# Gates of all rows at the end of the sample's attention, and the sample's recurrence products batch by batch

## The chip, the cores and the metric

The kernel runs on one core of a Trainium2 chip. What counts is the time of one execution on the device, in microseconds (us). The kernel before took 2453.69 us (median of 3 runs, 2449.02 to 2461.51).

The engines are named as the profile names them: PE (TensorE, matrix products; PEld its weight loads), DVE (VectorE), ACT (ScalarE), POOL (GpSimd) and SP (SyncE, which only starts DMA transfers here). Each works through its own queue in order and waits on semaphores for the others.

## What is computed

The reference is one inference step of a decoder layer for 256 prompt tokens and for a sample of 8 sequences with 4 new tokens each (288 rows in all, `NT`; 256 of them `NPR`). Cut to what matters here:

```python
# x @ w_in, split: RWKV-7 heads (16 x 64) | sparse attention heads (16 x 64, 4 KV heads)
g = jax.nn.sigmoid(gl) @ p['rwkv_g2']                    # gate, 160 -> 1024 columns
def step(S, inp):                                        # recurrence over tokens, S is 64 x 64 per head
    r_t, d_t, k_t, v_t, kk_t, a_t = inp
    sk = jnp.einsum('bhvk,bhk->bhv', S, kk_t)
    S = (S * d_t[:, :, None, :] - sk[..., None] * (kk_t * a_t)[:, :, None, :]
         + v_t[..., None] * k_t[:, :, None, :])
    return S, jnp.einsum('bhvk,bhk->bhv', S, r_t)
# y: group norm of the recurrence's rows, times g;  attention: compressed, selected and window branches
# x1 = LN1(ALPHA * x + concat(y, attention) @ w_out)
# PEER: q = x1 @ peer_wq, scores against two sets of 128 keys, the 16 best of the sums per head,
# out = sum over 8 heads x 16 experts of softmax * gelu(x1 . peer_u[e]) * peer_v[e];  LN2
```

## The kernel before

The code issues work in program order, and a scheduler with a cost model lays it out on the five queues. The function `weave` takes several generators, each with a number of units, and steps them in turn so that they advance in proportion; each generator says with `yield` where a unit ends. So the order around the change comes from the units given to `weave`, from buffer counts of the pools (a tile waits until the last reader of its buffer is done) and from `tc.issue_after(x)`, which ties instructions behind an instruction x in the schedule.

The stages, with the times that they have in the profile of before:

- **W3** (from about 575 to 758): `weave` of `late` (the sample's attention over its paged cache, 98 units: `sample_late`, in it 20 steps that load K and V into a ring of NCX = 10 buffers `co`, score, turn and apply them) with `sample_states` and `sample_steps` (54 units) and `outcomes`. `sample_states` loads the recurrent states of 8 sequences in two groups of four (16 DMAs each, L1240) and turns them (L1244) into `S0T`. `sample_steps` begins with the products of all states with the 4 tokens' rows, 128 small matmuls at L1259 (the profile records 256), copies them out in 16 pieces as `Ua` and `Ya`, solves the four steps, forms the new states (L1324 to L1327), turns them back (L1332) and writes them (L1337). The window's keys and values are loaded at L899.
- **W4** (to about 976): `weave` of the first units of `sample_chain`, of `prompt_attention` and of `out_first`. `sample_chain` multiplies the sample's gates (L1503, L1504), then its output product, its LN1, its wq and its scores with weights through a ring of NCW = 5 buffers `cw` (loads L1525, products L1527), and chooses its experts (L1362 to L1447). `prompt_attention` scores compressed blocks with small matmuls (L648) and then runs over blocks (scores L686, transposes L705, values L712, sums L717 and L721). `out_first` multiplies the prompt's gates (L1718 to L1720) and runs `out_part(0, BV)`, the half of the out product that takes the recurrence. The products of `out_part` are split into high and low parts: `YH`, `YL` (L1674, L1675) for the rows, `wh`, `wl` (L1684, L1685) for the weights, three matmuls each (L1690).
- **out** (to about 1059): the last units of `sample_chain` are `sample_dots`, NSD = 14 steps of two dots each: a gather of 128 half rows of an expert table (512 KB, POOL's queue, L453) into the ring `cw` and one DVE instruction (L1586). They are woven with `out_part(8, YN)`, the half that takes the attention.
- **ln1** (to about 1072): LN1 of the prompt's rows. `XT`, its transpose, is formed with gain and offset on ACT (L1767); the rows themselves get gain on DVE and offset on POOL (both L1782) and are written to memory as `x1d`. The remaining 18 steps of `sample_dots` (tile `sr`) begin here, NLD = 6 of them ahead of the gain and the offset, the rest in pairs under the heads of wq.
- **wq** and **peer** (to about 1700): queries (L1855; the weights come through L1741 into the rings `wraw` and `wraw2`), key scores (L1374 with the key table SKT, L1844), the choice per head, then expert dots from gathered rows (L1825) beside a dense product on PE (L1899). Behind them stand weigh and V.

## Time and profile before

| | us |
|---|---|
| median of 3 runs | 2453.69 |
| the profiled execution | 2450.29 |
| its span in the trace | 2448.5 |
| PE busy in it | 2255.8 (92%) |
| DVE busy | 1762.0 (72%) |
| POOL busy | 1332.6 (54%) |
| ACT busy | 823.4 (34%) |
| bytes moved by DMA | 684.07 MB, 279 GB/s over the span |

The mean granted clock of PE in that execution is 0.951 of full speed. In the rows of the profile a line such as "L1259 PE MATMUL ss<-sS,S0T" gives the line of the code, the engine, the operation and the tiles written and read; "x256" is a count, and a bracket such as "[5.08 <-DMA cw<-in_peer_u,ig]" says how long the engine was idle before the instruction and what ended the wait. SPq is SP's queue of transfers that it starts.

### The profile page before, as it was taken

To read this page: it belongs to the slowest core of one execution; us is meant where nothing else is said; L and a number is where in the kernel's file an instruction comes from. 1 tells how busy PE (TensorE), PEld (TensorE's weight loads), DVE (VectorE), ACT (ScalarE), POOL (GpSimd) and SP (SyncE) were. 2 spreads that over 40 slices of the span, in tenths; PEclk is the share of its full clock that TensorE was granted. 3 is DMA by queue.
4 is the path that set the end of the run, shared out by engine and by line. 5 is a ranking of instruction groups with operands and counts; after the bars stand their busy time and mean duration, and the time that the engine had idled before them with its cause. 6 is when DMAs were issued, how large, how long until landed. Compare 5 with 4: busy or idle time off the path is not lost.

```text
span 2448.5 us, 42558 instructions
## 1 busy us (share of the span) xinstructions
PE 2255.8 (92%) x15628; PEld 1888.4 (77%) x15628; DVE 1762.0 (72%) x4049; ACT 823.4 (34%) x1601; POOL 1332.6 (54%) x1347
## 2 busy tenths in 40 slices
PE   7988999897988998679999999999999899999996
PEld 7877889894645565558888888887777788887885
DVE  4788766555563355687877777556777899998888
ACT  4433222223432334221111111111777544444343
POOL 5687522324355011666766556565443688886772
PEclk9989999998896799789999999999999999999998
DMA  7777885448578784979999999999664799999994
GB/s 219 215 232 233 257 236 172 131 135 250 200 248 250 249 274 172 317 253 348 317 367 377 391 371 387 345 395 345 186 188 142 284 362 360 358 367 356 345 360 183
DMA packets 327600, 684.07 MB, mean 279 GB/s; under 512 B 82270, under 2 KB 200992, under 8 KB 326464
## 3 DMA queue, kind: packets, MB, share of 16 engines
q1 hardware_dynamic: 246176, 342.58, 42.2%
q0 software_dynamic: 81216, 338.78, 38.6%
q8 instruction: 123, 2.02, 0.3%
q14 instruction: 85, 0.70, 0.1%
HBM read 665.69 MB, written 23.88 MB: 282 GB/s over the span
## 4 chain that ended last, share of the span: by engine, by line
PE 29%; DMA 9%; DVE 8%; issue 7%; POOL 4%; ACT 1%; POOLq 0%; DVEq 0%; SPq 0%; ACTq 0%
PE pb L2107 20%; DMA rows<-in_peer_u_g,gi 8%; POOL rows L453 4%; PE px L1945 3%; DVE rows L1825 2%; PE pa L1978 2%; PE pj L1855 2%; PE pt L1937 1%; PE fs L1997 1%; DVE sr L1586 1%; DVE vl L2100 1%; DMA wraw<-in_peer_wq 0%; ACT vh L2099 0%; PE pa L1690 0%; DVE cw L1586 0%
## 5 line engine op out<-in xcount | busy, mean ns | idle before, releaser
L1899 PE MATMUL ph<-Xfd,ur 128*128 128x256 f32 x2304 | 497.6, 379 | 0.0
L1899 PEld LDWEIGHTS ph<-Xfd,ur 128*128 128x128 f32 x2304 | 437.6, 190 | 59.4
L453 POOL DMA_INDIRECT rq<-in_peer_v_g,gi x256 | 382.2, 1493 | 145.8 <-DVE fP L2080 85.6
L453 POOL DMA_INDIRECT rows<-in_peer_u_g,gi x256 | 313.3, 1224 | 189.3 <-DVE rows L1825 119.0
L1825 DVE SCALAR_TENSOR_TENSOR rows<-rows,x1a 128x896 f32<-128x896 f32 x256 | 278.8, 1097 | 136.2 <-DMA rows<-in_peer_u_g,gi 135.5
L422 PE MATMUL pj<-XH,wl 128*128 128x288 f32 (+1 forms) x752 | 233.5, 311 | 15.8 <-DVE wl L417 9.1
L422 PE MATMUL pj<-XH,wh 128*128 128x288 f32 (+1 forms) x752 | 232.1, 309 | 14.6 <-DVE ss L752 6.0
L422 PE MATMUL pj<-XL,wh 128*128 128x288 f32 (+1 forms) x752 | 228.0, 303 | 0.0
L2080 DVE SCALAR_TENSOR_TENSOR fP<-rq,ge,fP 128x640 f32<-128x640 f32 x254 | 223.7, 881 | 2.5
L2107 PE MATMUL pb<-vl,ah 128*128 128x512 f32 (+1 forms) x768 | 205.9, 376 | 0.8
L2107 PE MATMUL pb<-vh,al 128*128 128x512 f32 (+1 forms) x768 | 205.0, 375 | 0.0
L1900 ACT COPY AW<-ph 128x256 f32<-128x256 f32 x128 | 76.6, 612 | 370.5 <-PE ph L1899 362.7
L2107 PE MATMUL pb<-vh,ah 128*128 128x512 f32 (+1 forms) x768 | 185.6, 376 | 13.4 <-ACT vh L2099 10.9
L415 ACT CAST wh<-wraw 128x512 fp32r<-128x512 f32 (+1 forms) x188 | 115.1, 616 | 240.3 <-PE pj L422 191.1
L2107 PEld LDWEIGHTS pb<-vh,ah 128*128 128x128 f32 x768 | 144.1, 194 | 35.5 <-ACT vh L2099 13.9
L422 PEld LDWEIGHTS pj<-XH,wl 128*128 128x128 f32 (+1 forms) x752 | 145.8, 194 | 26.8 <-DVE wl L417 12.4
L476 DVE SCALAR_TENSOR_TENSOR CA<-co,wbc,CA 128x256 f32<-128x256 f32 x248 | 131.5, 568 | 46.5 <-DMA co<-in_cache_cmp_kv,gidx 46.5
L422 PEld LDWEIGHTS pj<-XH,wh 128*128 128x128 f32 (+1 forms) x752 | 146.1, 194 | 21.0 <-ACT wh L415 6.7
L2107 PEld LDWEIGHTS pb<-vl,ah 128*128 128x128 f32 x768 | 144.1, 194 | 22.7 <-DVE vl L2100 3.8
L2107 PEld LDWEIGHTS pb<-vh,al 128*128 128x128 f32 x768 | 144.5, 194 | 19.3
L422 PEld LDWEIGHTS pj<-XL,wh 128*128 128x128 f32 (+1 forms) x752 | 146.4, 195 | 1.5 <-issue 1.2
L417 DVE TENSOR_TENSOR wl<-wraw,wh 128x512 fp32r<-128x512 f32 (+1 forms) x141 | 100.8, 722 | 49.0 <-ACT wh L415 48.7
(871 smaller groups left out, 4335.6 us busy)
## 6 DMA issues: line engine op xcount, KB each, us to landing
ur<-in_peer_u_t SPq DMA_DIRECT2D x128, 576.0 KB
wraw<-in_w_in SPq DMA_DIRECT2D x152, 256.0 KB
cw<-in_w_out SPq DMA_DIRECT2D x32, 512.0 KB
wraw<-in_w_out SPq DMA_DIRECT2D x32, 512.0 KB
wraw<-in_peer_wq SPq DMA_DIRECT2D x32, 512.0 KB
cw<-in_peer_wq SPq DMA_DIRECT2D x32, 512.0 KB
wraw<-in_w_in SPq DMA_DIRECT2D x64, 128.0 KB
co<-in_state_win_kv SPq DMA_DIRECT2D x16, 512.0 KB
```

The costliest lines, as they stand in the source:

```text
L415: sc.copy(wh[:, :, :n], w[:, :, :n])
L417: i_ = en.tensor_tensor(wl[:, :, :n], w[:, :, :n], wh[:, :, :n].bitcast(F32), OP.subtract)
L422: last[2] = pe.matmul(pb[:n, :nt], wi[:, k, :n], xi[(o + k) // 8][:, (o + k) % 8, :nt], start=(o + k == 0 and wi is wh and xi is xh), stop ...
L453: gp.indirect_dma_start(out=dst, out_offset=None, in_=rows_, in_offset=bass.IndirectOffsetOnAxis(ap=ix, axis=0))
L476: ve.scalar_tensor_tensor(d_, x_, w_, d_, op0=OP.mult, op1=OP.add)
L1825: i_ = ve.scalar_tensor_tensor(r_, r_, 1.0, X1a[t], op0=OP.mult, op1=OP.mult, accum_out=h_)
L1855: pe.matmul(pb[:, :NPR], w[:, k, :], XT[:, o + k, :], start=(o + k == 0), stop=(o + k == 15))
L1899: mm = pe.matmul(ph[:, :NPR], w[:, e, :], Xfd[:, e, :], start=(e == 0), stop=(e == NDB - 1))
L1900: return mm, sc.copy(AW[:, i1 // 64, :, i1 % 64], ph[:, :NPR])
L1945: pin(pe.matmul(px[:, 128 * e:128 * e + 128].rearrange("p (c j) -> p c j", c=2), oT[:, e, :], AW[:, :, 4 * u + e, :], start=True, stop=True))
L2080: ve.scalar_tensor_tensor(fP[t], r_, w_, fP[t], op0=OP.mult, op1=OP.add)
L2107: pe.matmul(acc[3 * t + q][:, :n_], wi[:, P * t:P * t + P], xi[:, 512 * q:512 * q + n_], start=(k == 0 and wi is ah and xi is vh), stop=(k ...
```

## The change

Eight edits come together:

1. The gate products of the prompt's and the sample's rows, which were two sets of eight pairs of matmuls in W4 with two loads of the table `rwkv_g2`, become one set of eight pairs with 288 columns. It stands in W3, at the last but one steps of the sample's attention (the table is loaded at step 17 into the ring `co`, the products come at step 18). DVE multiplies the prompt's columns, ACT copies the sample's columns to a tile `Gs`, and DVE multiplies those after W3. The attention's units in `weave` go from 98 to 102, and W4's from 38 and 19 to 36 and 17.
2. The recurrence products move from `sample_steps` into `sample_states`: 16 matmuls behind each sequence's transposes, with one copy on DVE (`Ua`) and one on ACT (`Ya`) for each sequence.
3. The compressed scores of the prompt's attention are taken for two heads at once against a tile `cbz` with zeros in the other head's place: 8 matmuls of 16 columns for each half of the prompt where there were 16 of 8, one bank of PSUM where there were two, and two additions on DVE where there were four.
4. NSD goes from 14 to 10: four steps (eight gathers and eight dots) leave the chain and stand behind ln1.
5. In the out stage the sample's dots are tied behind the last low-part subtraction of `out_part` that has been issued on DVE (the list `lows`), and `out_part` stands ahead of the chain in `weave`.
6. In ln1 the offset goes from POOL to DVE, and the late dots stand behind the last offset, where they stood ahead of the first gain.
7. A spare tile of 768 columns stands ahead of SKT, so that SKT and `wraw2` lie at other addresses.
8. `Yv` takes the buffer of `Vc`.

The core of the diff (the scores, the tile lists and unchanged lines are left out):

```diff
-NSD = 14
+NSD = 10
...
+            if i == 17:
+                g2 = [co([P, 1024], "co", bufs=NCX) for _ in range(2)]
+                gate_rows(*g2)
+            if i == 18:
+                yield from gate_products(*g2)
...
+    def gate_products(g2a, g2b):
+        for j in range(8):
+            pb, js = bank("sa"), slice(128 * j, 128 * j + 128)
+            pe.matmul(pb[:, :NT], g2a[:, js], sg0, start=True, stop=False)
+            pe.matmul(pb[:, :NT], g2b[64:96, js], sg1[64:96, :], start=False, stop=True)
+            ve.tensor_tensor(BV[:, j, :NPR], pb[:, :NPR], BV[:, j, :NPR], OP.mult)
+            sc.copy(Gs[:, j, :], pb[:, NPR:NT])
+            yield 0.5
...
+            pb = bank("ss")
+            for ph in range(2):
+                for jj in range(4):
+                    for h in range(2):
+                        j = 4 * ((ph + h) % 2) + jj
+                        pe.matmul(pb[hs[h], 8 * j:8 * j + 8], S0T[hs[h], b, j, :], sPQ[hs[h], :, j, b::8],
+                                  start=True, stop=True)
+            v4 = pb[:, :64].rearrange("p (j q t) -> p q t j", j=8, q=2)
+            ve.tensor_copy(UY[0][:, :, :, b], v4[:, 0])
+            sc.copy(UY[1][:, :, :, b], v4[:, 1])
+            yield 1
...
-                ve.scalar_tensor_tensor(r_, r_, 1.0, x_, op0=OP.mult, op1=OP.mult, accum_out=h_)
+                with tc.issue_after(lows[-1].ins):
+                    ve.scalar_tensor_tensor(r_, r_, 1.0, x_, op0=OP.mult, op1=OP.mult, accum_out=h_)
...
-    weave((late, 98), (seq(sample_states(sx), sample_steps(sx)), 54), (outcomes(sx), 20))
+    weave((late, 102), (seq(sample_states(sx), sample_steps(sx)), 54), (outcomes(sx), 20))
+    ve.tensor_tensor(BV[:, :, NPR:], Gs, BV[:, :, NPR:], OP.mult)
...
-            ve.tensor_tensor(YL, src[:, q:q + 2, :NPR], YH.bitcast(F32), OP.subtract)
+            lows[:] = [ve.tensor_tensor(YL, src[:, q:q + 2, :NPR], YH.bitcast(F32), OP.subtract)]
...
+                if en is ve and cq + k > 2:
+                    lows[:] = [i_]
...
-    weave((take(chain, 38), 38), (prompt_attention(), 19), (out_first(), 19))
+    weave((take(chain, 36), 36), (prompt_attention(), 19), (out_first(), 17))
...
-    weave((chain, NSD), (out_part(8, YN), 16, 400))
+    weave((out_part(8, YN), 16, 400), (chain, NSD))
...
     with tc.issue_after(normed.ins):
-        for _ in take(late, NLD):
-            pass
...
-                        (ve if op_ is OP.mult else gp).tensor_tensor(x_, x_, y_, op_)
+                        offset = ve.tensor_tensor(x_, x_, y_, op_)
...
+    with tc.issue_after(offset.ins):
+        for _ in take(late, NLD):
+            pass
...
+    kq([P, 768], "spare")
```

What the scheduler makes of it is shown at three places. In these rows stand the line (of the kernel's own file, so lines of the changed kernel lie some 3 to 17 further down), the operation, the tile written, the tiles read and the shape; "x4" is a count of equal rows.

SP's queue in the second half of W3, before. `big` are the loaded states, `co` the window's keys and values, `out<-S` the new states written back, and `x_00` the first load of W4:

```order
L1240 DMA big<-in_state_rwkv 64x4x64 x16
L899 DMA co<-in_state_win_kv 128x1024 x8
L1337 DMA out<-S_9338 64x4x64 x4
L1337 DMA out<-S_9361 64x4x64
L899 DMA co<-in_state_win_kv 128x1024 x2
L1337 DMA out<-S_9361 64x4x64 x2
L899 DMA co<-in_state_win_kv 128x1024 x2
L1337 DMA out<-S_9361 64x4x64
L1337 DMA out<-S_9398 64x4x64 x4
```

The same place of the changed kernel:

```order
L902 DMA co<-in_state_win_kv 128x1024 x8
L1350 DMA out<-S_9391 64x4x64 x4
L1350 DMA out<-S_9420 64x4x64 x4
L1350 DMA out<-S_9453 64x4x64 x4
L1350 DMA out<-S_9490 64x4x64 x4
L1350 DMA out<-S_9511 64x4x64 x4
L902 DMA co<-in_state_win_kv 128x1024 x2
L1350 DMA out<-S_9555 64x4x64 x3
L902 DMA co<-in_state_win_kv 128x1024 x2
L1475 DMA co<-in_rwkv_g 128x1024
L1476 DMA co<-in_rwkv_g 32x1024
```

Before, five and seven of the 32 state writes stand ahead of the last two pairs of window loads and 25 behind them; now 20 and 23 stand ahead, and the gate table is loaded behind the last pair.

DVE where W4 passes into the out stage, before. The first row is the last step of the sample's choice, L1586 are the sample's dots:

```order
L1447 TENSOR_REDUCE EF<-cw 128x16
L1586 SCALAR_TENSOR_TENSOR cw,shT<-cw,x_10502 128x1024
L714 RECIPROCAL su<-su 128x8
L1577 TENSOR_SCALAR ig<-gi_72 128x32
L715 TENSOR_TENSOR su<-su,Gt 128x8
L1586 SCALAR_TENSOR_TENSOR cw,shT<-cw,x_10502 128x1024 x4
L717 TENSOR_TENSOR to<-sao,su 128x512
L1586 SCALAR_TENSOR_TENSOR cw,shT<-cw,x_10502 128x1024
L721 TENSOR_TENSOR O<-O,to 128x2x128
L1675 TENSOR_TENSOR YL_11558<-QT,YH_11557 128x512
L1586 SCALAR_TENSOR_TENSOR cw,shT<-cw,x_10502 128x1024
L1675 TENSOR_TENSOR YL_11562<-QT,YH_11561 128x512
```

The same place of the changed kernel (L1460 is the old L1447, L720 the old L717, L1684 the old L1675, L1591 the dots, L1695 the low part of the weights):

```order
L1460 TENSOR_REDUCE EF<-cw 128x16
L720 TENSOR_TENSOR to<-sao,su 128x512
L1581 TENSOR_SCALAR ig<-gi_72 128x32
L724 TENSOR_TENSOR O<-O,to 128x2x128 x2
L1684 TENSOR_TENSOR YL_11517<-QT,YH_11516 128x512
L1684 TENSOR_TENSOR YL_11521<-QT,YH_11520 128x512
L1684 TENSOR_TENSOR YL_11525<-QT,YH_11524 128x512
L1684 TENSOR_TENSOR YL_11529<-QT,YH_11528 128x512
L1591 SCALAR_TENSOR_TENSOR cw,shT<-cw,x_10509 128x1024 x4
L1695 TENSOR_TENSOR wl<-wraw,wh 128x1024
L1591 SCALAR_TENSOR_TENSOR cw,shT<-cw,x_10509 128x1024
```

The attention's last sum and the four low parts of its rows, which stood among twelve dots, now stand ahead of all of them.

SP's queue from ln1 into wq, before. SKT is the key table, the numbered `wraw` are weight loads of wq into `wraw2`'s buffers, and the plain `wraw` goes into the ring that PE reads first:

```order
L1752 DMA wraw<-in_ln_g 128x1024 x2
L1752 DMA wraw<-in_ln_b 128x1024 x2
L1741 DMA wraw<-in_peer_wq 128x8x128
L1844 DMA SKT<-in_subkeys_t 128x2048
L1741 DMA wraw_12195<-in_peer_wq 128x8x128
L1741 DMA wraw_12219<-in_peer_wq 128x8x128
L1741 DMA wraw_12249<-in_peer_wq 128x8x128
```

The same place of the changed kernel:

```order
L1756 DMA wraw<-in_ln_g 128x1024 x2
L1756 DMA wraw<-in_ln_b 128x1024 x2
L1850 DMA SKT<-in_subkeys_t 128x2048
L1745 DMA wraw_12150<-in_peer_wq 128x8x128
L1745 DMA wraw_12174<-in_peer_wq 128x8x128
L1745 DMA wraw_12204<-in_peer_wq 128x8x128
L1745 DMA wraw_12278<-in_peer_wq 128x8x128
L1745 DMA wraw<-in_peer_wq 128x8x128 x2
```

The load into the ring, which waits for PE's first product of wq, stood ahead of the key table; now the key table and four loads into buffers of their own stand ahead of it.

More of the change, by code (lines that the diff above doesn't have):

```diff
@@ L632, in prompt_attention @@
                          C2("hd").rearrange("p (k g) -> p k g", k=4)[:, :, :, None].to_broadcast([P, 4, 4, 64]), OP.mult)
+        cbz = np_([P, 2, 2, 8], "cbz")
+        gp.memset(cbz, 0.0)
+        for par in range(2):
+            gp.tensor_copy(cbz[hs[par], :, par, :], cb[0][hs[par]])
         for qt in range(2):
@@ L643, in prompt_attention @@
             Sc = np_([P, 2, 2, 4, 8], "Sc")
[L644 removed]
+            pb = bank("sa")
             for kp in range(2):
                 for g in range(4):
[L647 to L653 removed]
+                    o = 64 * kp + 16 * g
+                    pe.matmul(pb[:, o:o + 16], QT[:, kp, g, tok], cbz[:, kp].rearrange("p a n -> p (a n)"),
+                              start=True, stop=True)
+            for kp in range(2):
+                ve.tensor_tensor(Sc[:, kp], pb[:, 64 * kp:64 * kp + 64].rearrange("p (g a n) -> p a g n", g=4, a=2),
+                                 C2(f"cmpa{qt}")[:, None, None, :].to_broadcast([P, 2, 4, 8]), OP.add)
             S3 = Sc.rearrange("p a b g n -> p (a b g) n")
@@ L1219, in outcomes @@
             yield from outcome(s, 1, "ss", sp([P, 8, 64], "Y2", bufs=2, tag="PR"))
-    S0T = sPQ = sD = sBC = sUV = None
+    S0T = sPQ = sD = sBC = sUV = UY = None
     def sample_states(sp):
-        nonlocal S0T, sPQ, sD, sBC, sUV
+        nonlocal S0T, sPQ, sD, sBC, sUV, UY
         S0T, sS = sp([P, 8, 8, 64], "S0T"), sp([P, 8, 232], "sS")
+        UY = [sp([P, 4, 8, 8], nm) for nm in ("Ua", "Ya")]
         sPQ = sS[:, :, 0:64].rearrange("p j (q t) -> p q j t", q=2)
@@ L1497, in sample_chain @@
         ring = lambda: cx([P, 1024], "cw", bufs=NCW)
-        g2a, g2b = ring(), ring()
-        gate_rows(g2a, g2b)
-        pb = bank("ss")
-        for j in range(8):
-            o, js = pb[:, 32 * j:32 * j + 32], slice(128 * j, 128 * j + 128)
-            pe.matmul(o, g2a[:, js], sg0[:, NPR:], start=True, stop=False)
-            pe.matmul(o, g2b[64:96, js], sg1[64:96, NPR:], start=False, stop=True)
-        ve.tensor_tensor(BV[:, :, NPR:], pb[:, :256].rearrange("p (j t) -> p j t", j=8), BV[:, :, NPR:], OP.mult)
-        yield 1
         x1s, xr_, gs_, bs_ = (cx([P, 512], nm) for nm in ("x1s", "xr_", "gs_", "bs_"))
@@ L1667, in hybrid_decode_step @@
                 sy.dma_start(X1[t][h], a["x_prompt"][0, t * P:(t + 1) * P, 1024 * h:1024 * h + 1024])
+    lows = []
     def out_part(o, src):
@@ L1713, in out_first @@
         yield 1
-        g2a, g2b = (oe([P, 1024], "wraw", bufs=4) for _ in range(2))
-        gate_rows(g2a, g2b)
-        for j in range(8):
-            pb = bank("pa")
-            pe.matmul(pb[:, :NPR], g2a[:, 128 * j:128 * j + 128], sg0[:, :NPR], start=True, stop=False)
-            pe.matmul(pb[:, :NPR], g2b[64:96, 128 * j:128 * j + 128], sg1[64:96, :NPR], start=False, stop=True)
-            ve.tensor_tensor(BV[:, j, :NPR], pb[:, :NPR], BV[:, j, :NPR], OP.mult)
-        yield 2
         yield from out_part(0, BV)
     chain = sample_chain(cx[0])
-    weave((take(chain, 38), 38), (prompt_attention(), 19), (out_first(), 19))
+    weave((take(chain, 36), 36), (prompt_attention(), 19), (out_first(), 17))
     np_.close()
```

35 lines of the change are left out of this document (7 added, 28 removed).

## The prediction

> **What bounds the kernel now.** I first read the page's chain that ended last, then the table of stretches around the places that the change touches, then single rows. The chain's shares:
>
> ```profile
> PE 29%; DMA 9%; DVE 8%; issue 7%; POOL 4%; ACT 1%; POOLq 0%; DVEq 0%; SPq 0%; ACTq 0%
> ```
>
> No engine owns it, so the time has to be found stage by stage. In the table of stretches each row gives busy time (and count) of PE, PE's weight loads, DVE, ACT and POOL, then the granted clock, the DMA share and GB/s:
>
> ```profile
> 600.00:620.00 20.00, 15.48 (x177) 10.36 (x177) 9.68 (x37) 8.04 (x20) 8.39 (x10) 0.91 1.05 290
> 620.00:650.00 30.00, 29.17 (x391) 23.10 (x392) 6.76 (x29) 8.41 (x23) 5.72 (x6) 0.66 0.48 170
> 760.00:800.00 40.00, 38.30 (x148) 23.91 (x149) 10.86 (x31) 5.04 (x11) 24.11 (x47) 0.50 0.95 315
> 900.00:960.00 60.00, 57.66 (x474) 36.07 (x472) 26.14 (x87) 24.12 (x68) 2.40 (x1) 1.00 0.76 281
> 976.00:1008.00 32.00, 17.50 (x68) 14.21 (x68) 18.86 (x36) 8.77 (x19) 24.47 (x20) 0.65 0.81 256
> 1008.00:1059.00 51.00, 42.46 (x163) 32.12 (x164) 41.72 (x55) 12.64 (x12) 29.86 (x18) 0.93 0.91 330
> 1059.00:1072.00 13.00, 6.46 (x34) 5.80 (x32) 12.45 (x36) 5.68 (x17) 1.99 (x2) 0.74 0.05 17
> 1072.00:1090.00 18.00, 9.10 (x38) 7.56 (x39) 18.00 (x15) 6.00 (x18) 16.40 (x13) 0.82 0.94 306
> 1090.00:1202.00 112.00, 111.93 (x538) 98.79 (x537) 89.57 (x297) 12.91 (x32) 79.53 (x99) 0.98 1.07 355
> 1220.00:1700.00 480.00, 480.00 (x2228) 422.50 (x2227) 332.81 (x837) 78.13 (x137) 293.55 (x247) 1.00 0.98 374
> ```
>
> W4 (760 to 960) is PE: full at both ends, and its first 40 us run at half clock. The out stage (976 to 1059) is not PE but DVE and the DMAs. After a gap in ln1 the DMAs are full from 1072 to 1700, while PE is full from 1090. So a gain made before 1072 reaches the end only if both the PE work and the transfers behind it move up together.
>
> **The change part by part.** The sum is made against the profiled execution, 2450.29 us (span 2448.5), which lies 3.4 below the median 2453.69 of the three runs.
>
> *W3 (to about 758).* The recurrence products stand in one burst, at a clock of 0.50 to 0.83, in front of the attention:
>
> ```profile
> L1259 PE MATMUL ss<-sS,S0T x256: 199/251/273, 622.1 to 647.1; 64*64 64x8 f32 x128
> 723.68 4.46 SPq L1337 DMA_DIRECT2D out<-S  x5
> 728.33 0.97 SPq L899 DMA_DIRECT2D co<-in_state_win_kv  x2
> 732.30 25.81 SPq L1337 DMA_DIRECT2D out<-S  x25
> 761.92 1.63 SPq L1525 DMA_DIRECT2D cw<-in_w_out  x3
> ```
>
> Spread batch by batch they are the same 128 matmuls, but most of them run before the last states are loaded and turned, where PE has room (15.48 of 20 us busy in 600 to 620). Of the 25 us from 622.1 to 647.1 I leave the last batch, 25 / 8 = 3, and some crowding, so that the recurrence ends an estimated 10 to 20 us earlier. Against that stand eight pairs of gate products of 288 columns. W3 has none of that shape; the nearest rows are the 256-column pairs below, which took 1.06 to 1.22 us at half clock and 0.70 at the end: two matmuls at about 0.35 each, 8 × 2 × 0.35 = 5.6, with 288 columns some 6 to 8 us of PE. DVE gets the multiplications that it had. Net I take −4 for the end of W3. Bounds: −10 (the recurrence's tail of 25 state writes, 25.81 us of SP's queue, no longer stands in front of W4's first loads) and +14 (in the new order 20 state writes stand ahead of the last four window loads, where it were five to seven; at 25.81 / 25 = 1.03 us each these may come 13 to 15 us later).
>
> *W4.* Groups of PE between 755 and 960:
>
> ```profile
> L648 PE MATMUL sa<-cb,QT 64*128 64x8 f32 x64 | 11.2, 307 | 0.0
> L1719 PE MATMUL pa<-sg,wraw 32*128 32x256 f32 x16 | 8.6, 631 | 0.0
> L1718 PE MATMUL pa<-sg,wraw 128*128 128x256 f32 x16 | 8.4, 624 | 0.0
> L1503 PE MATMUL ss<-sg,cw 128*128 128x32 f32 x16 | 5.1, 411 | 0.4 <-DMA cw<-in_rwkv_g 0.4
> L1504 PE MATMUL ss<-sg,cw 32*128 32x32 f32 x16 | 5.1, 407 | 0.3 <-DMA cw<-in_rwkv_g 0.3
> ```
>
> The gate products of L1503/L1504 and L1718/L1719 leave W4: 5.1 + 5.1 + 8.4 + 8.6 = 27.2 us. The scores of L648 go from 64 recorded matmuls to 16 of twice the columns: at 307 ns each 4.9, so −6.3. Together 33.5 us of PE, nearly all of it at half clock: the prompt's gate products alone stretch from the first of these rows to the second, where the out product gets its turn.
>
> ```profile
> 782.83 1.22 PE L1718 MATMUL pa<-sg,wraw 128*128 128x256 f32 x2
> 807.64 0.50 PE L1690 MATMUL pa<-wh,YH 128*128 128x512 f32 x1
> ```
>
> If the half clock is a stretch of time (40 us whatever stands in it), other work takes the place and runs slowly there: the gain is then half, 17 us; if it ends with the same amount of work, 33. I take 18, the nearer to the lower end, because the row at 760 to 800 shows a busy PE held at 0.50. The clear bounds are 10 and 30. That the chain's loads follow PE and not the other way round is read from SP's waits between 730 and 960:
>
> ```profile
> SPq L1525 <- PE ss L1527: 84.0, 44, 7.5
> ```
>
> 84 us of waiting for a ring buffer that PE had not read yet: a sooner PE gets sooner loads. On the clock the Trainium skill ("TensorE: Matmul & The Clock Gate", Part 1, What's actually happening) says that the clock returns to full after one window of about 3.4 us of sustained work. The trace differs: 0.50 over 40 us in which PE was busy for 38.30. By the page only a few microseconds of W4 would run slowly in the changed kernel, and the sum would come out some 15 us lower; I go by the trace.
>
> *Out stage.* The sample's expert dots (L1586) begin when its experts are chosen, at 976.4, and hold DVE's queue while they wait for their gathers; the prompt attention's tail and the low parts of the out product stand behind them:
>
> ```profile
> L1586 DVE SCALAR_TENSOR_TENSOR cw<-cw,x x28: 1203/1217/3408, 976.4 to 1057.8; 128x1024 f32<-128x1024 f32 x28
> ...
> 983.09 1.23 DVE L1586 SCALAR_TENSOR_TENSOR cw<-cw,x 128x1024 f32<-128x1024 f32 x1 [5.08 <-DMA cw<-in_peer_u,ig]
> ...
> 989.87 0.69 DVE L717 TENSOR_TENSOR to<-sao,su 128x512 f32<-128x512 f32 x1
> ...
> 1003.65 1.23 DVE L1586 SCALAR_TENSOR_TENSOR cw<-cw,x 128x1024 f32<-128x1024 f32 x1 [4.90 <-DMA cw<-in_peer_u,gi]
> 1004.80 0.69 DVE L1675 TENSOR_TENSOR YL<-QT,YH 128x512 fp32r<-128x512 f32 x1
> ...
> 1007.91 1.22 DVE L1685 TENSOR_TENSOR wl<-wraw,wh 128x1024 fp32r<-128x1024 f32 x1
> ```
>
> So the out product begins 1007.9 − 976.4 = 31.5 us after the choice. In the new order L717, L721 and all four L1675 stand ahead of the first dot, and four dots (4 × 1.22 = 4.9) ahead of the first L1685: with the tail's own 2 × 0.69 + 4 × 0.69 and its steps on PE and ACT, I estimate 12 us. Twenty dots instead of 28 remain. By DVE the stage is then 12 + 51 (the stretch after 1008 holds 16 dots today, and 16 of 20 would be left) = 63. By bytes: 32 × 256 + 51 × 330 = 25.0 MB today, less 8 gathers of 512 KB = 20.8 MB, at 330 GB/s 63 us. Today it is 83; both give −20. Bounds −10 (the new wait: dots tied behind the subtractions keep their five ring buffers, POOL's next gathers wait for those, and the transfers start some 10 us late) and −30 (the eight dots and the wait gone in full).
>
> *ln1 and the start of wq.* SP's queue holds a weight load that waits for PE's first product, ahead of the key table and of the loads needed next:
>
> ```profile
> 1072.43 7.17 PE L1855 MATMUL pj<-XT,wraw 128*128 128x256 f32 x32 [1.22 <-ACT XT L1767]
> ...
> 1076.18 0.38 SPq L1741 DMA_DIRECT2D wraw<-in_peer_wq  x1
> 1076.61 0.57 SPq L1844 DMA_DIRECT2D SKT<-in_subkeys_t  x1
> ...
> 1087.56 1.19 PE L1374 MATMUL pb<-SKT,QP 128*128 128x128 f32 x4 [7.95 <-DMA SKT<-in_subkeys_t]
> 1089.27 3.35 PE L1855 MATMUL pj<-XT,wraw 128*128 128x256 f32 x7 [0.52 <-DMA wraw<-in_peer_wq]
> ```
>
> PE stops at 1072.43 + 7.17 = 1079.6 and goes on with weights at 1089.27: 9.7 us. In the new order the key table and four loads stand ahead of the load that waits, and none of these five needs PE's wq products, so they can use the idle DMAs of 1059 to 1072. I take −9.7 for PE; at worst 0. The offsets of ln1 that move from POOL to DVE are eight instructions of 512 columns; today eight products on DVE run beside the offsets on POOL:
>
> ```profile
> 1073.94 13.20 DVE L1782 TENSOR_TENSOR x<-x,wraw 128x512 f32<-128x512 f32 x8
> ```
>
> Sixteen alone at the 0.69 of an L717 are 11 us: no more than the 13.20 that eight take beside POOL, and PE waits for XT, not for these. I cost it at nothing; without that cover it is −2 (11 − 13.2) to +11.
>
> *What comes back later.* Four steps of the sample's dots (8 gathers of 512 KB, 4.2 MB, and 8 dots, 9.8 us of DVE) move from the out stage into wq and peer, where the DMAs are full: 4.2 MB at 355 GB/s are 11.8 us. Bounds are 0 (hidden in ln1's gap) and 21.6 (both added). The peer stage shows who waits there:
>
> ```profile
> L1899 PE MATMUL ph<-Xfd,ur 128*128 128x256 f32 x2304 | 497.6, 379 | 0.0
> L1825 DVE SCALAR_TENSOR_TENSOR rows<-rows,x1a 128x896 f32<-128x896 f32 x256 | 278.8, 1097 | 136.2 <-DMA rows<-in_peer_u_g,gi 135.5
> ```
>
> PE never idles in it and the row dots wait 135.5 us for gathers: PE and the transfers end it together. PE's path gains 4 + 18 + 20 + 9.7 = 51.7. The transfers' path gains 4 + 18 + 20, and up to 13 of ln1's gap, less 11.8: 43.2. The end goes with the slower: I take −44, **2406 us**.
>
> **The rivals.**
> 1. *W4 is set by its transfers.* For it: DMA shares of 0.95 and 0.76, and the chain streams about 50 MB. Against it: the 84 us above. If so, only the two double loads of the gate table (1.3 MB, at 315 GB/s 4 us) are saved there: −44 + 14 = −30, 2420; with a W3 at its bound of +14 it is 2438.
> 2. *The saturated stretch gives it back.* The row gathers begin when heads are chosen; with four more dots in each of two more heads on DVE and 4.2 MB more ahead of them, PE comes early and the rows don't. Then the peer stage ends with the row dots: of the 42 gained before ln1, 11.8 for bytes and 9.8 for DVE are lost and nothing of the gap is won: −20, 2430.
> 3. *The low clock spreads (slower).* The clock fell to 0.66 and 0.50 exactly where PE had small or narrow matmuls after idle time. Batchwise products put such matmuls over the whole of 580 to 640, and W4 begins with narrow ones again. Each microsecond at 0.50 costs half of one. It decides when the low stretches are longer by (44 + 12) × 2 = 112 us in all; with 140 us more the time is 2450 − 44 + 70 = 2476. Against it: each low stretch shown ends within 40 us.
> 4. *The change doesn't do what it says:* the dots stand behind the subtractions, but the attention's tail is itself late, so that the out product begins no sooner after the choice and its stage keeps its length: 2406 + 20 = 2426. For it: PE's last attention product of today came 9.7 us after the choice.
>
> ```profile
> 986.11 1.06 PE L712 MATMUL sao<-vw,PTs 128*128 128x64 f32 x4
> ```
>
> Against it: today DVE's last row maximum of the attention stands just ahead of the choice's last step, and in the new order it stands ahead of the whole second half of the choosing; how many microseconds that is, the order doesn't say.
>
> **How the numbers follow.** My forecast, 2390 to 2420, gets 0.50; below 2390 (the half clock ends with its work, −15, and the out stage at its −30) 0.12; rival 1 0.14; rival 2 0.14; rival 4 0.05; rival 3 0.05. The bounds of the terms add up to −10 − 30 − 30 − 9.7 = −80 and, the other way, to +14 − 10 − 10 + 21.6 = +16, which would take all of them at once. The range 2376 to 2442 leaves out about 0.2: its lower end is the forecast with −15 for the clock and −15 for the out stage and the bytes, its upper end takes in rivals 1, 2 and 4. A measurement here tells 0.5%, 12 us, from no change: faster means below 2441. Faster 0.86, same 0.08, slower 0.06.
>
> **What would show it.** In the changed profile: no burst at half clock in 620 to 650, and the last state write well before the end of W3; the chain's last w_out and wq product about 20 us sooner than the end of W4 today; 12 us, not 31.5, between the choice and the first low part of the out product; PE without a gap of 9.7 us between its first and second wq column; and the scores' end and the row dots' end both some 40 us earlier. The forecast is wrong if W3 ends later than 765, if the low clock lasts past 40 us, or if the last row dot ends much later than PE's last peer product.

## The result, and the profile after

| | us |
|---|---|
| changed kernel, median of 13 runs | 2461.17 (2453.32 to 2481.66) |
| kernel before in the same comparison, median of 13 | 2448.91 (2438.19 to 2464.73) |
| ratio, 95% interval | 1.0061 (1.0032 to 1.0089) |
| profiled execution of the changed kernel | 2468.68, span 2466.9 |

The forecast was 2406: in this comparison the change costs 0.6% where a gain of 1.8% was expected. First the table of stretches of the changed kernel, with the columns that the prediction used:

```profile
760.00:800.00 40.00, 36.39 (x237) 20.65 (x236) 21.19 (x67) 13.73 (x37) 18.73 (x38) 0.79 0.71 237
1008.00:1059.00 51.00, 36.76 (x144) 27.31 (x144) 43.82 (x74) 11.10 (x12) 21.20 (x13) 0.92 0.87 290
1059.00:1072.00 13.00, 10.98 (x61) 9.91 (x60) 13.00 (x23) 13.00 (x35) 1.18 (x2) 0.93 0.64 185
1072.00:1090.00 18.00, 18.00 (x89) 15.96 (x88) 10.44 (x19) 2.08 (x6) 10.64 (x11) 1.00 0.97 326
1090.00:1202.00 112.00, 111.93 (x546) 99.13 (x545) 99.78 (x322) 9.92 (x27) 87.79 (x103) 1.00 1.04 346
1202.00:1220.00 18.00, 0.63 (x3) 0.20 (x2) 13.98 (x33) 0.00 (x0) 15.50 (x12) 0.66 0.75 252
1220.00:1700.00 480.00, 461.90 (x2134) 406.35 (x2135) 325.59 (x809) 78.60 (x137) 271.89 (x243) 0.98 0.96 369
```

PE's gap in ln1 and wq is closed (18.00 of 18.00 from 1072 to 1090, where it was 9.10), but a new hole has opened: from 1202 to 1220 PE works for 0.63 of 18 us and ACT for none. The costliest group of the page says who ends it, and how long it was in all:

```profile
L1905 PE MATMUL ph<-Xfd,ur 128*128 128x256 f32 x2304 | 499.7, 380 | 35.5 <-ACT AW L1906 35.5
```

`AW` is the tile into which ACT copies the dense product's banks. Before, this group (L1899) had 0.0 idle. How the kernel stood at the start of the peer stage is read from the timelines of the three engines; first the changed kernel, PE, ACT, then DVE (start, length, what was done, and in brackets the idle time before it with its releaser):

```profile
1183.04 19.59 PE L1905 MATMUL ph<-Xfd,ur 128*128 128x256 f32 x90
1238.10 22.14 PE L1905 MATMUL ph<-Xfd,ur 128*128 128x256 f32 x93 [35.47 <-ACT AW L1906]
...
1221.77 0.31 ACT L1468 ACTIVATE ge<-ge 128x128 f32<-128x128 f32 x1 [38.11 <-DVE ge L1467]
1237.44 2.39 ACT L1906 COPY AW<-ph 128x256 f32<-128x256 f32 x5 [15.36 <-DMA rows<-in_peer_u_g,gi]
...
1235.99 1.22 DVE L1591 SCALAR_TENSOR_TENSOR sr<-sr,sx 128x1024 f32<-128x1024 f32 x1
```

PE fills its five banks in 19.59 us and then stands until ACT has emptied one. ACT's first copy comes 0.2 us after the end of the last of the sample's 44 late dots (1235.99 + 1.22 = 1237.2). The releaser named there is a transfer; the row of the kernel with NSD = 10 alone, below, names the dots. The same place of the kernel before:

```profile
1202.26 58.01 PE L1899 MATMUL ph<-Xfd,ur 128*128 128x256 f32 x268
...
1209.31 1.21 DVE L1586 SCALAR_TENSOR_TENSOR sr<-sr,sx 128x1024 f32<-128x1024 f32 x1
...
1210.69 1.07 ACT L1900 COPY AW<-ph 128x256 f32<-128x256 f32 x2 [7.80 <-DVE TF L1407]
```

There too the first copy follows the last dot, by 0.2 us (1209.31 + 1.21 = 1210.5), and comes 8.4 us after PE's first product. (The releaser named there is a small cast that DVE does right behind the dot.) In all 20 profiles of this case the first copy begins 0.16 to 0.24 us behind the end of the last late dot. The banks would have been full at 1202.26 + 19.59 = 1221.85: a margin of 11.2 us, which no idle time shows. `AW` lies in memory that the late dots' pool gave back (in the code its pool opens on the side where the pool of `sr` has just been closed), so its first writer waits for that pool's last reader. Now there are 22 late steps of two dots instead of 18, the last four of them behind heads 7 and 8, and the margin is gone.

The marks of the two profiles, and of a second pair that ran later, both on one chip (two of the experiments):

| us | before | changed | difference | before, second pair | changed, second pair | difference | forecast |
|---|---|---|---|---|---|---|---|
| end of W3 (last turn of the sample's attention) | 755.6 | 781.7 | +26.1 | 755.6 | 751.9 | −3.7 | −4 |
| experts chosen | 976.5 | 981.4 | +4.9 | 969.7 | 964.5 | −5.2 | −22 |
| last out product begins | 1058.6 | 1050.5 | −8.1 | 1050.7 | 1033.9 | −16.8 | −42 |
| first peer product | 1202.3 | 1183.0 | −19.3 | 1195.7 | 1166.4 | −29.3 | −52 |
| last peer product | 1699.8 | 1718.1 | +18.3 | 1693.2 | 1702.1 | +8.9 | −44 |
| span | 2448.5 | 2466.9 | +18.4 | 2441.7 | 2450.2 | +8.5 | −44 |

In both pairs the changed kernel is ahead at the peer stage, by 19 and by 29 us, and gives back 38 us in it.

### The profile page after: what moved, and what is told of

Same layout as the page of the kernel before. It is cut to its first block, busy times and chain, and to the rows that moved or that the text cites. A ratio compares the mean times of both kernels' runs of the same rounds, so it can differ in the third digit from the quotient of the medians.

```text
span 2466.9 us, 42414 instructions
## 1 busy us (share of the span) xinstructions
PE 2248.0 (91%) x15564; PEld 1875.6 (76%) x15564; DVE 1763.5 (71%) x4053; ACT 826.1 (33%) x1609; POOL 1295.7 (53%) x1342
## 4 chain that ended last, share of the span: by engine, by line
PE 69%; DVE 10%; DMA 8%; issue 5%; POOL 5%; ACT 2%; SPq 0%; another core or an unknown queue 0%; DVEq 0%; POOLq 0%; ACTq 0%
PE ph L1905 19%; PE pb L2113 18%; PE pj L422 6%; PE px L1951 3%; PE pa L1984 2%; DMA co<-in_cache_cmp_kv,gidx 2%; PE pj L1861 2%; PE pa L1702 2%; PE sa L923 2%; PE p L1096 2%; PE pt L1943 2%; DMA rows<-in_peer_u_g,gi 1%; PE fs L2003 1%; DVE CA L476 1%; PE ss L1531 1%
## 5 line engine op out<-in xcount | busy, mean ns | idle before, releaser
L1905 PE MATMUL ph<-Xfd,ur 128*128 128x256 f32 x2304 | 499.7, 380 | 35.5 <-ACT AW L1906 35.5
L453 POOL DMA_INDIRECT rows<-in_peer_u_g,gi x256 | 295.6, 1155 | 221.2 <-DVE rows L1831 147.8
L422 PE MATMUL pj<-XH,wh 128*128 128x288 f32 (+1 forms) x752 | 229.8, 306 | 13.9 <-DVE ss L755 6.8
L2113 PEld LDWEIGHTS pb<-vh,ah 128*128 128x128 f32 x768 | 144.7, 195 | 35.8 <-ACT vh L2105 13.9
L422 PEld LDWEIGHTS pj<-XH,wl 128*128 128x128 f32 (+1 forms) x752 | 144.2, 192 | 26.3 <-DVE wl L417 12.2
L2113 PEld LDWEIGHTS pb<-vh,al 128*128 128x128 f32 x768 | 144.4, 194 | 19.3
```

The lines of the kernel that those rows point to most:

```text
L422: last[2] = pe.matmul(pb[:n, :nt], wi[:, k, :n], xi[(o + k) // 8][:, (o + k) % 8, :nt], start=(o + k == 0 and wi is wh and xi is xh), stop ...
L453: gp.indirect_dma_start(out=dst, out_offset=None, in_=rows_, in_offset=bass.IndirectOffsetOnAxis(ap=ix, axis=0))
L1905: mm = pe.matmul(ph[:, :NPR], w[:, e, :], Xfd[:, e, :], start=(e == 0), stop=(e == NDB - 1))
L2113: pe.matmul(acc[3 * t + q][:, :n_], wi[:, P * t:P * t + P], xi[:, 512 * q:512 * q + n_], start=(k == 0 and wi is ah and xi is vh), stop=(k ...
```

## The experiments

Each ratio is to the kernel before, run on the same chip at the same time.

### The peer stage: which edit stalls it

The changed kernel with the fourth edit undone:

```diff
-NSD = 10
+NSD = 14
```

> The changed kernel with NSD back at 14, so that 36 late dots stand behind ln1 as before the change, not 44. Theory L (late dots): the peer stage's result tile AW lies in the memory of the late dots' ring, so its first copy waits for the last late dot (1237.1 in the changed kernel), and PE, with five banks filled, stands 35.5 us. Then the 35.5 us wait is gone (under 3 us), the out stage is up to 10 us longer for its eight dots, and the time is 20 to 35 us below the changed kernel's 2461: 2426 to 2441. Rival D: the peer stage's end is set by the row gathers, and PE's wait only shows it; then the last row dot stays at about the same distance from the scores' end (1707 - 1183 = 524) and the time within 8 us of 2461.

Measured: 2440.31 us, 0.9976 (0.9946 to 1.0006). The last row dot begins 504.8 us after the first peer product (1175.8 to 1680.6), not 524, so rival D fails. The stall is gone:

```profile
L1905 PE MATMUL ph<-Xfd,ur 128*128 128x256 f32 x2304 | 497.6, 379 | 0.0
```

The fourth edit alone, on the kernel before (`NSD = 14` to `NSD = 10`):

> The kernel before with NSD at 10 alone: 44 late dots stand behind ln1. Theory L: the last late dot moves from 1209 to about 1236 on the clock of the kernel before, where PE's five banks are full at 1222, so PE stands 10 to 25 us in the peer stage; the out stage gains about 10: time within 5 below to 18 above the kernel before. Rival: the stall in the changed kernel needs PE's early start, and here there is none (under 3 us): time 5 to 12 below.

Measured: 2475.66 us, 1.0076 (1.0046 to 1.0106). The group of the dense product, and ACT's first copy with its releaser:

```profile
L1899 PE MATMUL ph<-Xfd,ur 128*128 128x256 f32 x2304 | 499.3, 380 | 28.3 <-ACT AW L1900 28.3
...
1248.57 2.39 ACT L1900 COPY AW<-ph 128x256 f32<-128x256 f32 x5 [13.02 <-DVE sr L1586]
```

Here the trace names the dots (`sr`, L1586) as what ACT waited for. One edit makes the stall, with nothing else of the change in the kernel: the theory of the late dots, L in the expectations, holds, though stall and time (23 us above the kernel before) are larger than it said. Still, both runs move 4.2 MB and eight dots together with the place of the last dot. The next run keeps the bytes and moves the place only: ten of the 22 late steps stand ahead of the heads, so the last pair stands under head 6, as before the change. It ran beside the kernel with NSD = 14 again.

```diff
-NLD = 6
+NLD = 10
```

> The changed kernel with NLD = 10: the sample's same 22 late steps (44 dots, the same bytes) stay behind ln1, but ten of them instead of six stand ahead of the heads, so that the last pair stands under head 6, as before the change, and not under head 8. Theory M (the stall is a wait for memory: the first copy into AW needs the buffer that the last late dot reads): the first AW copy comes within 20 us of the first peer product, PE's idle time at L1905 falls from 36 to under 5 us, and the time is 0.4 to 1.2% below the changed kernel's, near the kernel with NSD = 14. Theory B (the stall is what 4.2 MB and eight dots more cost in wq and peer, wherever they stand): PE's wq or peer stage together stay within 5 us of the changed kernel's 652 us from the first wq product to the last peer product, whether the idle time is seen at L1905 or moves ahead into wq, and the time is within 0.3% of the changed kernel's.

> The changed kernel with NSD = 14 once more, on the chip of the run with NLD = 10, as its yardstick: 36 late dots. Theory M: PE idle 0.0 at L1905, ratio to the kernel before 0.995 to 1.000, and the run with NLD = 10 within 0.4% of it. Theory B: the run with NLD = 10 is 0.6 to 1% slower than this one, as the changed kernel was against the first run of this one.

Measured: 2417.29 us, 0.9896 (0.9847 to 0.9945), and with NSD = 14 2418.49 us, 0.9891 (0.9831 to 0.9950). The kernel with NLD = 10 has all 44 dots behind ln1 and almost no stall (its first copy still comes 22.3 us after the first peer product, where theory M allowed 20):

```profile
L1905 PE MATMUL ph<-Xfd,ur 128*128 128x256 f32 x2304 | 499.5, 380 | 3.3 <-ACT AW L1906 3.3
```

From the first wq product to the last peer product it takes 1036.2 to 1658.9, 622.7 us; the changed kernel 1064.9 to 1718.1, 653.2 us. So on PE it is the place of the last late dots that costs 30 us, not their bytes: theory M, which is L made narrower. What the bytes cost shows behind the dense product, where PE now waits for the last row dots; first with NLD = 10, then the first run with NSD = 14:

```profile
1673.57 0.47 PE L1846 MATMUL pb<-CT,hd 128*128 128x128 f32 x1 [14.00 <-DVE rows L1831]
```

```profile
1681.78 0.48 PE L1846 MATMUL pb<-CT,hd 128*128 128x128 f32 x1 [7.76 <-DVE rows L1831]
```

Without the stall the row dots end last, by 7.8 us (9.5 in the second run with NSD = 14), and with eight more late gathers by 14.0. The stall had hidden that the transfers were next, and so not all of the 30 us reaches the stage behind. From the first wq product to this product of L1846 it takes 653.7 and 654.3 us in the two profiles of the changed kernel, 637.4 with NLD = 10, and 626.5 with NSD = 14 on the same chip. Counted there, the place costs 16 us and the eight late gathers with their dots 11.

### The other edits one by one

The gates alone (edits 1 and 8 on the kernel before):

> The kernel before with the gates' move alone (and the buffer of Vc reused for Yv, which makes room for Gs). Theory R (the recurrence batch by batch is what lengthens W3): the attention's last transpose comes at 755.6 plus the 8 pairs of gate products, about 764, and the start of the out stage some 10 us earlier than before: time 5 to 15 us below before. Rival G (the gate products and their table lengthen W3 themselves): last transpose at 772 or later, time equal to before or up to 10 above.

Measured: 2443.44 us, 0.9962 (0.9933 to 0.9990). W3 ends at 764.5, the experts are chosen at 961.4, so W4 takes 196.9 us where it took 220.9 (214.1 in the second profile of the kernel before): −17 to −24. The gate products cost W3 about 5 us: its last quarter takes 39.3 us, 34.4 in the kernel before.

The recurrence products alone (edit 2):

> The kernel before with the recurrence products batch by batch alone. Theory R: 20 state writes go ahead of the last four window loads, which come about 15 us later, and the attention's last transpose comes 10 to 20 us after 755.6; time 8 to 20 us above before. Rival G: last transpose at 745 to 757 and time 0 to 10 below before.

Measured: 2461.38 us, 1.0045 (1.0020 to 1.0069). W3 ends at 775.2. The burst is gone from the trace, and nothing is won by it: time and W3 come out as theory R said, whose reason, the state writes, is tried below. (The profiled execution took 2483.79 us and was the slowest of ten.)

The tie alone (edit 5):

> The kernel before with the tie of the dots behind the low parts, and the out product ahead of the chain in the weave, alone. Theory T (the order on DVE was what delayed the out product): first low part of the weights 10 to 16 us after the choice, where it was 31.5, the out stage from the choice to the last out product 8 to 15 us shorter than 82, time 4 to 14 us below before. Rival B (the gathers' transfers set the stage): the stage stays within 4 us of 82 and the time within 4 of before.

Measured: 2451.04 us, 0.9981 (0.9958 to 1.0004). From the choice to the last out product are 75.6 us (82.1 before), but the first low part of the weights still comes 20.4 us after the choice, where theory T asked for 10 to 16.

The offset on DVE with the late dots behind it (edit 6, without the spare tile):

> The kernel before with the offset of ln1 on DVE and the late dots behind it, alone. Theory S (SP's queue): the key table and four loads go ahead of the load that waits for PE, PE's 9.7 us gap between the first and second column of wq is under 3 us, and the time 5 to 12 us below before. Rival D: the transfers behind are the limit, the gap comes back as waits for weights later in wq or for rows in peer, and the time is within 4 us of before.

Measured: 2444.80 us, 0.9967 (0.9939 to 0.9996). PE in ln1 and wq of this kernel:

```profile
1068.54 20.99 PE L1856 MATMUL pj<-XT,wraw 128*128 128x256 f32 x96 [2.08 <-ACT XT L1767]
1089.36 1.05 PE L1374 MATMUL pb<-SKT,QP 128*128 128x128 f32 x8
```

The wait of 9.7 us for the weights behind the key table is gone: the queries run from 1068.5 to 1185.2, 116.7 us, where they took 128.4.

### Versions without the fourth edit

The changed kernel with NSD = 14 and the recurrence's burst of before (edit 2 undone, edit 3 kept):

```diff
-NSD = 10
+NSD = 14
...
-            v4 = pb[:, :64].rearrange("p (j q t) -> p q t j", j=8, q=2)
-            ve.tensor_copy(UY[0][:, :, :, b], v4[:, 0])
-            sc.copy(UY[1][:, :, :, b], v4[:, 1])
...
+            v5 = bk[q][:, :256].rearrange("p (j b q t) -> p q t j b", j=4, b=8, q=2)
+            for t in range(4):
+                ve.tensor_copy(Ua[:, t, 4 * q:4 * q + 4, :], v5[:, 0, t])
+                sc.copy(Ya[:, t, 4 * q:4 * q + 4, :], v5[:, 1, t])
```

> The changed kernel with NSD at 14 and with the recurrence products in one burst as before the change. Theories L and R together: no long wait in the peer stage, last transpose of the attention at about 764, 10 to 18 us below the run with fourteen steps and the products batch by batch: 2410 to 2428, below both kernels. Rival G: as long as that run, within 5 us.

Measured: 2477.65 us, 1.0115 (1.0075 to 1.0156): far from every expectation. The end of W4 in this kernel:

```profile
900.00:940.00 40.00, 38.47 (x329) 23.17 (x327) 20.68 (x99) 17.04 (x62) 0.66 (x4) 1.00 0.59 205
940.00:1000.00 60.00, 47.05 (x172) 36.19 (x172) 26.17 (x115) 19.00 (x60) 11.96 (x20) 0.51 0.13 44
```

The chain's products end at 930.1; the prompt's attention is left over, runs alone in small steps at a clock of 0.51 until 1009, and the dots tied behind the out product's low parts wait for it. The same kernel without edit 3, that is the kernel before with the gates, the tie, the offset, the spare tile and `Yv`:

> The kernel before with the gates' move, the tie of the dots, the offset on DVE and the spare tile: of the change without the batchwise recurrence, the joined scores and NSD. If the gains are those of W4, of the out stage and of wq's start, and the losses those of the recurrence (10 us) and of NSD (20 us), it is 15 to 30 us below before: 2420 to 2434, the best of all. If the scheduler again lets the prompt's attention fall behind the chain, the out product begins after 1000 and the time is 2440 or more.

Measured: 2432.91 us, 0.9926 (0.9900 to 0.9953); the same on another chip, later:

> Gates, offset and tie with the products in one burst, on the same chip. By both theories last transpose 6 to 10 us after that of the kernel before.

Measured: 2421.88 us, 0.9933 (0.9900 to 0.9967). The two kernels differ by the joined scores alone, and by 45 us, though on two chips. The attention's last value product begins at 1009.4 in one and at 967.7 in the other. The scores save PE some microseconds, but the schedule that they give leaves the attention behind. Adding the batchwise recurrence to it:

> The run with gates, offset and tie, and the recurrence products batch by batch on top. Theory O (what is left for W3: the recurrence's state updates, pulled forward, stand among the attention's work in its second and third quarter and leave PE alone with a chain of waits later): third quarter 52 to 57 us, last transpose 772 to 780, time 6 to 14 us above that run's 2433. Rival: the cost of the recurrence edit belonged to the other parts of the change; time within 4 of 2433.

Measured: 2419.81 us, 0.9943 (0.9911 to 0.9974). W3 ends at 756.0, not at 772 to 780 as theory O asked. This is the kernel with NSD = 14 above less the joined scores; that one's 0.9976 and 0.9891 lie on both sides of it, so beside the batchwise recurrence no harm of the scores shows in the time.

### Why W3 ended 26 us later

Theory W: 20 state writes stand ahead of the last window loads in SP's queue. In the changed kernel:

```profile
718.63 23.88 SPq L1350 DMA_DIRECT2D out<-S  x20
745.60 1.27 SPq L902 DMA_DIRECT2D co<-in_state_win_kv  x2
```

The writes were put on POOL's queue, in the kernel with NSD = 14:

```diff
-                    sy.dma_start(nrw[b, jp, h], S1
+                    gp.dma_start(nrw[b, jp, h], S1
```

> The run with fourteen steps (all of the change but NSD) with the recurrence's state writes issued by POOL, so that SP's last four window loads and the gate table stand behind no write. Theory W (the writes ahead of them in SP's queue lengthen W3): window loads by 735, the attention's last transpose at 755 to 764, time 6 to 15 below that run's 2440. Rival O (the order of the recurrence's pieces on PE, ACT and DVE, and the clock, lengthen it): last transpose at 767 or later and time within 5 of 2440.

Measured: 2458.29 us, 1.0025 (0.9993 to 1.0056), and W3 still ends late, at 778.5. Then 28 of the 32 writes were left out:

> The run with fourteen steps (all of the change but NSD), in which 28 of the 32 new states are formed but not written back, so that SP's window loads have four writes ahead of them and no other engine gets any. By the attention's four quarters (its transposes of a finished pair): theory W (the writes in SP's queue lengthen the third quarter): the third quarter is 44 to 50 us where that run has 53.7, the last transpose comes at 760 to 766 and W3 is 6 to 12 us shorter than that run's 771.9. Rival O (the recurrence's pieces on PE, ACT and DVE, pulled forward into that quarter, lengthen it): third quarter 52 to 57, last transpose at 769 to 780.

Measured: 2444.79 us, 0.9955 (0.9925 to 0.9984). SP's queue, and W3's end is 774.3 all the same:

```profile
714.91 2.61 SPq L1350 DMA_DIRECT2D out<-S  x4
738.68 3.88 SPq L902 DMA_DIRECT2D co<-in_state_win_kv  x4
```

A late W3 does not need the writes. Theory O, that the state updates' matmuls crowd the attention's third quarter:

```diff
-                pe.matmul(pb[hs[h], :], BCt[:, j, 64 * h:64 * h + 64], uvm
+                with tc.issue_after(ends[1].ins):
+                    pe.matmul(pb[hs[h], :], BCt[:, j, 64 * h:64 * h + 64], uvm
```

> The same with the state updates' products on PE tied behind the end of the attention's second quarter, where they stand by themselves in the kernel before. Theory O: third quarter 44 to 50 us, last transpose 763 to 770, time within 4 us of the run with the burst (2433) and 5 to 12 below the run without the tie. Rival P (the products themselves, 14 us in the first quarter, are the cost, wherever the updates stand): third quarter unchanged or the second longer by as much, last transpose 772 or later, time as without the tie within 4.

Measured, on the kernel of the last run of the part above: 2412.79 us, 0.9889 (0.9854 to 0.9924). But the third quarter takes 49.4 us (49.0 without the tie) and the two spans are 2412.9 and 2412.0: the profile does not show what the theory asked for, and why the median is lower stays open. Last, four kernels on one chip, to ask whether there is a W3 effect at all: the kernel before itself, the changed kernel itself, the burst version (all but edits 2, 3 and 4) and the batchwise version (all but edits 3 and 4).

> The kernel before, profiled on the same chip as the next three. If its last attention transpose comes at about 755 to 765 here too, the earlier profiles of different chips may be compared within some 5 us; if it comes near 740, this chip's W3 is shorter by itself, and only the differences inside this group count.

> The changed kernel on the same chip. Theory C (the change itself lengthens W3 by 17 to 26 us, gates 7, recurrence 10 or more): last transpose 17 to 26 us after that of the kernel before in this group. Rival J (much of the 26 us was the chip or the execution): 5 to 14 us after it, by the gate products and little else. Peer stall 30 to 37 us by either.

> The same with the products batch by batch. Theory C: last transpose 8 to 14 us after that of the burst, time 6 to 14 us above it. Rival J: within 5 us of it, both.

| kernel, on one chip | ratio | W3 ends | experts chosen | first peer product | span |
|---|---|---|---|---|---|
| before | 1.0018 (0.9995 to 1.0042) | 755.6 | 969.7 | 1195.7 | 2441.7 |
| changed | 0.9995 (0.9967 to 1.0023) | 751.9 | 964.5 | 1166.4 | 2450.2 |
| burst | 0.9933 (0.9900 to 0.9967) | 760.1 | 952.3 | 1158.9 | 2418.4 |
| batchwise | 0.9951 (0.9919 to 0.9984) | 758.6 | 956.7 | 1161.7 | 2419.0 |

Here the changed kernel's W3 ends earlier than that of before, earlier even than rival J in the expectations allowed, and the batchwise W3 as early as the burst's. The batchwise version's median, 2429.24 us, is 7.4 above the burst's, as theory C had it, but the intervals overlap. So the edit need not cost W3 anything. On three other chips batchwise kernels ended W3 at 771.9 to 778.5, on two more at 750.6 to 756.0.

The two profiles of the changed kernel, which are of one program, show where they part. The same piece of work takes 60 us in the second and 74.9 in the first:

```profile
570.00:630.00 60.00, 57.04 (x736) 40.52 (x734) 33.34 (x143) 27.90 (x69) 17.68 (x18) 0.89 0.71 214
```

```profile
572.60:647.50 74.90, 68.14 (x734) 47.01 (x726) 33.64 (x143) 27.57 (x69) 17.67 (x18) 0.75 0.56 169
```

DVE, ACT and POOL are equally busy in both; PE is busy 11.1 us longer, at a granted clock of 0.75 instead of 0.89. In a second such place, 699 to 716 against 718.4 to 744.7, 5.0 of 9.3 us are PE's, at 0.87 instead of 1.00. So 16 of the 30 us between the two ends of W3 are PE's busy time at a lower clock. Why the clock was lower in one of them was not found. In both, 20 state writes stand ahead of the last window loads, which also speaks against theory W. The stall is there again:

```profile
PE ph L1905 <- ACT AW L1906: 36.4, 1, 36.4
```

This row of the waits (total, times, longest) belongs to the changed kernel's second profile. That profiled execution took 2452.02 us, 14 above the kernel's own median of 2437.73: a span of one execution says less than the marks within it.

## Why the prediction was wrong

**The step that failed** is "What comes back later". It priced the four moved steps by bytes (11.8 us) and by DVE's time (9.8 us), with 0 to 21.6 as bounds, and read from "PE never idles in it" that only PE's work and the transfers could set the peer stage. The runs show a wait on top of them: the place of the last late dot decides when ACT may first write `AW`, and PE stops when its five banks are full. The stall is 35.5, 36.4 and 28.3 us in the three kernels with NSD = 10 and NLD = 6, 3.3 with NLD = 10, and 0.0 with NSD = 14. Before, the margin was 11.2 us. The forecast had +8 for this step on its way from −52 to −44; the measured return is 38. The work itself was priced about rightly: once the stall is gone, the eight late gathers cost 11 us. In the second pair, where W3 ended as forecast, the forecast misses by 52 us: 30 of them lie in this step, 17 in W4 and 8 in the out stage, and ln1 and wq gave 3 back.

- **W3, −4.** In the first profile +26.1, in the second −3.7. The gate products cost the last quarter some 5 us, near the 6 to 8 worked out, but that sum misread the rows: the profile records each of these matmuls twice (as it records the 128 of L1259 as 256), so the row of 0.70 us is one matmul and sixteen are 11 us. PE was busy with them for 5.9 + 6.0 us in the first profile. The batchwise order shows no gain: 1.0045 alone, and 0.9951 against 0.9933 beside the burst on one chip, where the intervals overlap. The upper bound's mechanism, SP's state writes, is not the cause. W3 of the batchwise kernels ends anywhere between 750.6 and 781.7; in the one pair compared above, the granted clock makes 16 us of it, and the rest stays open.
- **W4, −18.** The gates alone made it 17 to 24 us shorter and the burst version 22 (192.2 where it was 214.1), of 27.2 us of PE time that left it, so the half clock's share was guessed too low. In the changed kernel it is −21.2 in the first pair, behind a late W3, and −1.5 in the second. By the marks, what counts is the choice of the experts: −22 forecast, +4.9 and −5.2 measured, −17.4 without edits 2, 3 and 4. The term of the joined scores, −6.3, was a saving in PE time alone, and a little less: the rows go from 64 to 32, not 16, and from 11.2 us to 5.6 and 7.2. It does not show in the stage: W4 takes 190.7 to 198.1 us in the six profiles that have the first edit without the scores, and 196.1 to 213.1 in the seven batchwise ones with them. In the burst kernel edit 3 cost 45 us by the order that the schedule made of it; in the changed kernel its share was not measured alone on one chip.
- **Out stage, −20.** −13.0 and −11.6. The wait between choice and first low part became 14.8 us, not 12, near the estimate. The eight dots' share was mis-sized: with them back (NSD = 14) the stage takes 70.7 us, without them 69.1, so they are worth 1.6 us once they stand behind the subtractions. The sum by bytes, 20.8 MB at 330 GB/s, fell with its rate: 330 is that of the stage's second half, and over the whole stage the DMAs moved 303 GB/s before and 298 in the changed kernel, at which 20.8 MB take 70 us. By time, then, the fourth edit bought 1.6 us for a stall of 35.5.
- **ln1 and wq, −9.7.** Right in mechanism and size: −11.2 and −12.5 from the last out product to the first peer product, −9.7 of it the wait for weights. The edit that does it is the sixth. The offsets cost next to nothing, as said: from the last out product to the first wq product it takes 14.4 us in both profiles, 13.8 and 13.9 before.
- **Rival 2,** "The saturated stretch gives it back", had the right stage with the wrong mechanism as long as the stall was there. With the stall removed its mechanism appears: PE ends 7.8 to 14 us before the row dots. **Rival 4** was refuted: the dots do stand behind the subtractions and the out product begins sooner. **Rival 3** is not what made it slower as a whole: the mean granted clock is 0.948, 0.951 before. But part of it is there, in W3 of the first profile.
- **Slower at 0.06** was too small a chance, though the second comparison shows no slowing (0.9995), because each price of a moved step was work; none was a wait that the trace of before had hidden. It did show the place: the copy L1900 0.2 us behind the last late dot.

The change without its fourth edit, or with `NLD = 10` beside it, does much of what was forecast (0.9891 and 0.9896 on one chip; 0.9976 for the former on another). The fastest against the kernel before, at 0.9889 (0.9854 to 0.9924), leaves out edits 3 and 4 and ties the state updates; its interval overlaps theirs.

## What to carry to other kernels

Work that is moved later holds its memory longer: before it is priced by its duration, ask which tile takes that memory next, which engine writes it first, and how many buffers the engine behind that one can fill meanwhile. An engine with 0.0 idle time still has a margin, which is read from the timelines as the distance between a buffer's release and the moment at which it would be missed. And a stage that differs by 26 us between two single profiles is compared once more on one chip, and by its granted clock, before it is explained.

## What the runs showed of the hardware

The clock stays low for longer than the idle time that goes before it. In the changed kernel PE is full from 700 to 710 and still runs at half clock, after 3.37 us without work; in the kernel with NSD = 14 it runs at half clock for some 16 us, busy for 12.2 of them, after the wait of 7.76 us for the row dots:

```profile
699.76 0.63 PE L552 MATMUL sa<-im,CT 128*128 128x32 f32 x2 [3.37 <-DVE im L549]
...
700.00:710.00 10.00, 10.00 (x37) 5.40 (x38) 4.16 (x16) 1.16 (x4) 0.00 (x0) 0.50 0.33 132
```

```profile
1682.00:1690.00 8.00, 5.81 (x24) 4.78 (x24) 4.96 (x12) 1.75 (x3) 5.46 (x5) 0.50 0.78 238
1690.00:1698.00 8.00, 6.43 (x27) 5.27 (x26) 5.51 (x21) 3.84 (x8) 0.00 (x0) 0.50 0.40 157
```

The Trainium skill ("TensorE: Matmul & The Clock Gate", Part 1, What's actually happening) has the clock fall after an idle window of about 3.4 us, which agrees with the first of these rows, and rise after as long a sustained one, which the second does not show: 10.00 us of 10 were busy at 0.50. A wait thus costs more than its own length: behind the 7.76 us the turns and products of the next stage took up to twice their time (2.08 us where the same eight take 1.16 further on):

```profile
1684.82 2.08 PE L1951 MATMUL px<-AW,oT 128*128 128x128 f32 x8 [0.72 <-ACT oT L1945]
...
1701.39 1.16 PE L1951 MATMUL px<-AW,oT 128*128 128x128 f32 x8
```

The changed kernel is 1.0061 (1.0032 to 1.0089) in one comparison and 0.9995 (0.9967 to 1.0023) in another, each beside the kernel before. The intervals do not overlap, so even a ratio with a narrow interval does not carry from one comparison to another here to better than about 0.7 of a per cent; smaller differences between experiments on different chips are not to be read.
